# S5 matrices and rotation tables computed in the retention passes and reloaded per step

## The chip, the cores and the metric

The kernel runs on one core of a Trainium2 chip, as one launch. The metric is device time in microseconds (us); three runs of the kernel before gave 1194.45, 1194.66 and 1196.43, and 1194.66 is their median. Five engines work beside each other, each through its own instructions in order: TensorE (PE, with its weight loads as PEld), VectorE (DVE), ScalarE (ACT), GpSimd (POOL) and SyncE (SP), which here issues the DMAs.

## The reference

One block on x of 1024 x 1024 (sequence x model), float32, cut to what matters:

```python
h = rms_norm(x, norm1_g)
q, k, v, g_ret, u, g_s5 = split(h @ w_in)            # widths 512, 512, 4 x 1024
ret = retention(rotary(q), rotary(k), v, ret_gn_g) * silu(g_ret)   # 8 heads, chunks of 128
# S5 branch: 64 groups of 16 channels, 64 complex states each
dt = exp(log_dt);  abar = exp(a * dt)                # per group and state
bb = (abar - 1) / a * b
x_t = abar * x_(t-1) + bb @ u_t                      # associative scan over the sequence
y = gelu(Re(c @ x_t) + d * u)
y = y * sigmoid(y @ glu_w + glu_b)
x = x + concat(ret, y * silu(g_s5)) @ w_out
x = x + cross_attention(rms_norm(x), rms_norm(mem))  # 256 memory rows, 4 heads
out = rms_norm(x)
```

The recurrence of the S5 branch depends on the inputs only through u. Everything made from a, dt, b, c and d alone (the powers of abar, the input matrix, the output matrix, the local kernel) can be computed without u.

## The kernel before

The program runs through stages: loading and norm (to about 37 us), four retention passes i = 0 to 3 of two heads each, the S5 stretch, then the gate (`glups`), the second half of the output projection (`obps`), cross attention and its output (`wops`). A matrix product in full precision is three matmuls (`mm3`: high x high, high x low, low x high; L95 to L97), so a projection tile of 128 output columns over the whole sequence is 48 matmuls of 512 columns, into one of two large PSUM buffers (tag `big`); four small PSUM buffers (tag `sm`) serve everything else. Each weight block is loaded by SP, its high half `whi` made by ScalarE and its low half `wlo` by GpSimd for `w_u`, `w_gs` and `w_oa`, by VectorE otherwise; both have two buffers.

A retention pass projects k and q (`kps`, `qps`), v (`vps`) and the gate (`gps`), then runs `retention()`: scores and states (`st`, `R`), the outputs `ops`, the group norm (`ve`, three Newton steps `t_gn`, `nb`), the normalisation of `o` on ScalarE (L480), the product with the gate on VectorE (L481), the transposes `rtps` on TensorE and a store of `rt` to DRAM. The rope of q and k needs half rows swapped, which SP does by DMA (`sw_k`, `sw_q`).

The S5 stretch (about 370 to 720 us) projects u (`ups`, 8 tiles, each evacuated as `ut` and stored), the S5 gate (`gsps`, 8 tiles) and the first half of the output projection (`oaps`, 8 tiles, on `reth` and `retl`, the halves of the stored retention output). Beside these tiles stand the steps of the S5 branch, for b = 0 to 15 (four groups each): `s5_step()` emits `s5_out(b-2)`, `s5_state(b-1)` and `s5_prep(b)`.
- `s5_prep(b)` makes, on GpSimd, for every second b (each `ct`) the rotation tables `tab` by doubling; per b the small tiles B1, B2, C1 and `t1`; on VectorE the matrix W1 (L568, L570) and the output matrix VV (L577 to L579); on TensorE the transposes `mps` of W1 and the local kernel `kps` (L582); on ScalarE the copies Mi, `ktz` and the per-b copy CS of the tables (L597). Eight DMAs build Dm from `ktz`.
- `s5_state(b)` multiplies u by Mi (`Sps`), rotates (S, Sw) and scans (X); `s5_out(b)` rotates back (X2), multiplies by Dm and VV (`yps`), applies gelu and stores `yy`.

`s5_params()`, the powers of abar and the tables' start, is emitted in pass 1. A scheduler orders the instructions of every engine by a simulated timeline; each engine then runs its list in order and waits on semaphores, and a tile with one buffer makes its next writer wait for its last reader. SP's list is in order as well, so a store whose data is late holds the loads behind it.

Of the kernel before, what the change touches and what calls it, by code (L numbers as in the profile page):

```python
# [45 lines left out]
def block_kernel(ctx: ExitStack, tc: tile.TileContext, a: dict):  # L46
# [473 lines left out]
    NB = G // GB  # L520
    dms = []
    for z in range(2):
        dm = sb.tile([P, 2 * GB, P], F32, name=f"Dm{z}")
        g.memset(dm, 0.0)
        dms.append(dm)
    per_ct = {}

    def s5_prep(b):
        gs = slice(b * GB, b * GB + GB)
        ct, hb = b // 2, b % 2  # L530
        if hb == 0:
            raw = sb.tile([P, 2, 4, GB, 16], F32, tag="bcraw", name=f"bcraw{ct}", bufs=2)
            nc.sync.dma_start(out=raw, in_=a["s5_bc"][ct])
            tab = sb.tile([P, 2, GB, SC], F32, tag="tab", name=f"tab{ct}", bufs=2)
            g.tensor_copy(tab[:, 0, :, 0:16], rotC[:, ct])
            g.tensor_copy(tab[:, 1, :, 0:16], rotS[:, ct])
            scr = sb.tile([P, 256], F32, tag="tg", name=f"tg{ct}", bufs=1)
            rotate_double(tab[:, 0], tab[:, 1], 16, SC, scr, 4)
            ktz = sb.tile([16, 2 * GB, P], F32, tag="ktz", name=f"ktz_{ct}", bufs=1)
            per_ct[ct] = raw, tab, ktz  # L540
        raw, tab, ktz = per_ct[ct]
        raw = raw[:, hb]
        ks = slice(hb * GB, hb * GB + GB)
        B1 = sb.tile([P, GB, 16], F32, tag="B1", name=f"B1_{b}", bufs=2)
        B2 = sb.tile([P, GB, 16], F32, tag="B2", name=f"B2_{b}", bufs=1)
        C1 = sb.tile([P, GB, 16], F32, tag="C1", name=f"C1_{b}", bufs=1)
        tt = sb.tile([P, GB, 16], F32, tag="tt16", name=f"tt16_{b}", bufs=1)
        sh = [P, GB, 16]

        def fb(x):  # L550
            return bc(x[:, gs].unsqueeze(2), sh)
        g.tensor_tensor(B1, raw[:, 0], fb(FR), ALU.mult)
        g.tensor_tensor(tt, raw[:, 1], fb(FIs), ALU.mult)
        g.tensor_tensor(B1, B1, tt, ALU.add)
        g.tensor_tensor(B2, raw[:, 1], fb(FRs), ALU.mult)
        g.tensor_tensor(tt, raw[:, 0], fb(FI), ALU.mult)
        g.tensor_tensor(B2, B2, tt, ALU.subtract)
        g.tensor_scalar(C1, raw[:, 2], psgn, None, op0=ALU.mult)

        def pw(tab, n):  # L560
            return bc(tab[:, 0:n, gs].rearrange("p t g -> p g t").unsqueeze(3), [P, GB, n, 16])

        def ve(x, n):
            return bc(x.unsqueeze(2), [P, GB, n, 16])
        W1 = sb.tile([P, GB, 8, 16], F32, tag="W1", name=f"W1_{b}", bufs=1)
        t1 = sb.tile([P, GB, 9, 16], F32, tag="t1", name=f"t1_{b}", bufs=1)
        VV = sb.tile([P, GB, 9, 16], F32, tag="VV", name=f"VV_{b}", bufs=3)
        v.tensor_tensor(W1, pw(PR, 8), ve(B1, 8), ALU.mult)  # L568
        g.tensor_tensor(t1[:, :, 0:8], pw(PI, 8), ve(B2, 8), ALU.mult)
        v.tensor_tensor(W1, W1, t1[:, :, 0:8], ALU.add)  # L570
        mp = sm_ps([P, GB, P], "mps")
        for gi in range(GB):
            nc.tensor.transpose(mp[:, gi, :], W1[:, gi].rearrange("p t q -> p (t q)"), ident)
# [1 line left out]
        s.activation(Mi, mp, AF.Copy)
        t2 = sb.tile([P, GB, 9, 16], F32, tag="t1", name=f"t2_{b}", bufs=1)
        v.tensor_tensor(VV, pw(PR, 9), ve(C1, 9), ALU.mult)  # L577
        v.tensor_tensor(t2, pw(PI, 9), ve(raw[:, 3], 9), ALU.mult)
        v.tensor_tensor(VV, VV, t2, ALU.subtract)  # L579
        kp = sm_ps([P, P], "kps")  # L580
        for gi in range(GB):
            nc.tensor.matmul(kp[32 * gi:32 * gi + 16, :], B1[:, gi, :], VV[:, gi, 0:8, :].rearrange("p t q -> p (t q)"),  # L582
                             start=True, stop=True)
        for gi in range(GB):
            s.activation(ktz[:, hb * GB + gi, :], kp[32 * gi:32 * gi + 16, :], AF.Copy)
        dd = sb.tile([16, GB, 16], F32, tag="dd", name=f"dd_{b}", bufs=1)
        g.tensor_tensor(dd, bc(i16.unsqueeze(1), [16, GB, 16]), bc(d16[:, gs].unsqueeze(2), [16, GB, 16]), ALU.mult)
        g.tensor_tensor(ktz[:, ks, 0:16], ktz[:, ks, 0:16], dd, ALU.add)
        Dm = dms[ct % 2]
        if hb == 1:  # L590
            for j in range(8):
                r = 7 - j
                nc.sync.dma_start(out=Dm[16 * r:16 * r + 16, :, j * 16:P], in_=ktz[:, :, 0:P - j * 16])
        r0 = 64 * hb
        CS = sb.tile([P, 2, GB, SC], F32, tag="CS", name=f"CS_{b}", bufs=2)
# [495 lines left out]
```

## Time and profile before

| | |
|---|---|
| median of three runs | 1194.66 us |
| profiled execution | 1195.26 us, its span 1193.5 us |
| mean granted TensorE clock | 0.988 |
| busy: TensorE, VectorE, ScalarE, GpSimd | 1147.6, 677.6, 497.7, 297.9 us |
| chain that ended last | PE 73%, DVE 10%, POOL 5% |
| DMA | 137.67 MB, mean 115 GB/s |

The span is the time between the first and the last instruction; the device time has 1.8 us around it. The busy share is an average over stages with different limits, so the rows below are taken by stretch. Matmuls overlap in the records: one of 512 columns is noted with about 0.4 us, but the next starts 0.23 us later.

### The profile page before, as it was taken

The page shows a single profiled execution, that of the slowest core. Times are in us where ns is not written, and L with a number is a line of the kernel's source. Part 1 is how long each engine was busy: PE and PEld are TensorE (multiplying, and loading weights), DVE is VectorE, ACT ScalarE, POOL GpSimd, SP SyncE. Part 2 cuts the span into 40 slices and gives each one's busy share as a digit, 9 for nine tenths or more (in the row PEclk, how much of TensorE's full clock was granted, in tenths as well). Part 3 has the DMA queues.
Part 4 walks back from the last instruction along what each step waited for, and adds up shares of the span by engine and source line. Part 5 has one row for each costly group of instructions (what it writes and reads, how often), then busy time and mean ns, then how long its engine had stood idle before and what let it go on. Part 6 is the DMA issues. An engine that isn't in the chain of part 4 may idle for free.

```text
span 1193.5 us, 18220 instructions
## 1 busy us (share of the span) xinstructions
PE 1147.6 (96%) x7020; PEld 997.4 (84%) x7020; DVE 677.6 (57%) x1388; ACT 497.7 (42%) x983; POOL 297.9 (25%) x432
## 2 busy tenths in 40 slices
PE   9899999999999998899979999999999999999996
PEld 6898998998988877777757787888889988889996
DVE  8964414415114388999889746544545445554564
ACT  7322531522523135656655425223324444444452
POOL 1430000000112698889985200000330000000000
PEclk9899999999999998999989999999999999999999
DMA  6411311212211524343454459534444622222251
GB/s 218 114 37 54 89 54 37 98 62 55 88 54 54 176 72 127 122 125 110 149 160 160 125 187 284 173 124 135 134 150 164 206 76 72 71 71 71 90 194 71
DMA packets 74070, 137.67 MB, mean 115 GB/s; under 512 B 13952, under 2 KB 39808, under 8 KB 73984
## 3 DMA queue, kind: packets, MB, share of 16 engines
q1 hardware_dynamic: 73696, 136.38, 35.6%
q8 instruction: 55, 0.90, 0.3%
q14 instruction: 31, 0.25, 0.1%
q10 hardware_dynamic: 288, 0.14, 0.0%
HBM read 100.57 MB, written 29.36 MB: 109 GB/s over the span
## 4 chain that ended last, share of the span: by engine, by line
PE 73%; DVE 10%; POOL 5%; issue 4%; ACT 3%; DMA 3%; SPq 1%; DVEq 0%; ACTq 0%; POOLq 0%
PE vps L95 3%; PE vps L96 3%; PE vps L97 3%; PE gps L96 3%; PE wops L97 3%; PE wops L95 3%; PE wops L96 3%; PE gps L95 3%; PE gps L97 3%; PE glups L96 2%; PE qaps L97 2%; PE qaps L95 2%; PE qaps L96 2%; PE glups L97 2%; PE obps L96 2%
## 5 line engine op out<-in xcount | busy, mean ns | idle before, releaser
L75 POOL TENSOR_TENSOR wlo_w_u<-wraw_w_u,whi_w_u 128x512 fp32r<-128x512 f32 x16 | 20.7, 1325 | 286.2 <-ACT whi_w_u L74 286.2
L95 PE MATMUL wops<-whi_w_xo,o 128*128 128x256 f32 x256 | 74.1, 289 | 0.0
L95 PE MATMUL vps<-whi_w_v,hh 128*128 128x256 f32 x256 | 73.3, 286 | 0.6 <-ACT qs_k L288 0.6
L96 PE MATMUL vps<-wlo_w_v,hh 128*128 128x256 f32 x256 | 73.6, 287 | 0.0
L97 PE MATMUL vps<-whi_w_v,hl 128*128 128x256 f32 x256 | 73.4, 287 | 0.0
L97 PE MATMUL wops<-whi_w_xo,o 128*128 128x256 f32 x256 | 72.5, 283 | 0.0
L96 PE MATMUL wops<-wlo_w_xo,o 128*128 128x256 f32 x256 | 72.4, 283 | 0.0
L96 PE MATMUL gps<-wlo_w_g,hh 128*128 128x256 f32 x256 | 72.0, 281 | 0.0
L97 PE MATMUL gps<-whi_w_g,hl 128*128 128x256 f32 x256 | 72.0, 281 | 0.0
L95 PE MATMUL gps<-whi_w_g,hh 128*128 128x256 f32 x256 | 72.0, 281 | 0.0
L821 POOL TENSOR_TENSOR sq<-sq,sqx 128x1024 f32<-128x1024 f32 x7 | 19.1, 2723 | 190.2 <-ACT sqx L820 190.2
L95 PE MATMUL gsps<-hh,whi_w_gs 128*128 128x512 f32 x128 | 51.2, 400 | 7.3 <-DVE ut L678 7.3
L96 PE MATMUL oaps<-retl,whi_w_oa 128*128 128x512 f32 x128 | 51.9, 405 | 4.2 <-DVE retl L705 4.2
L95 PE MATMUL oaps<-reth,whi_w_oa 128*128 128x512 f32 x128 | 52.0, 408 | 0.0
L97 PE MATMUL oaps<-reth,wlo_w_oa 128*128 128x512 f32 x128 | 51.7, 404 | 0.0
L96 PE MATMUL gsps<-hl,whi_w_gs 128*128 128x512 f32 x128 | 51.3, 401 | 0.0
L96 PE MATMUL glups<-yl,whi_w_glu 128*128 128x512 f32 x128 | 50.7, 397 | 0.6 <-DVE yl L743 0.6
L97 PE MATMUL gsps<-hh,wlo_w_gs 128*128 128x512 f32 x128 | 51.1, 399 | 0.0
L96 PE MATMUL ups<-hl,whi_w_u 128*128 128x512 f32 x128 | 50.9, 398 | 0.0
L97 PE MATMUL ups<-hh,wlo_w_u 128*128 128x512 f32 x128 | 50.8, 397 | 0.0
L95 PE MATMUL ups<-hh,whi_w_u 128*128 128x512 f32 x128 | 50.8, 397 | 0.0
L95 PE MATMUL qaps<-h,whi_w_xq 128*128 128x512 f32 x128 | 50.7, 396 | 0.0
(395 smaller groups left out, 3627.2 us busy)
## 6 DMA issues: line engine op xcount, KB each, us to landing
yr<-y_d SPq DMA_DIRECT2D x16, 512.0 KB, 6.7
wraw_w_xq<-w_xq SPq DMA_DIRECT2D x16, 512.0 KB, 4.2
wraw_w_xo<-w_xo SPq DMA_DIRECT2D x16, 512.0 KB, 4.3
wraw_w_v<-w_v SPq DMA_DIRECT2D x8, 512.0 KB, 4.1
wraw_w_g<-w_g SPq DMA_DIRECT2D x8, 512.0 KB, 4.8
ret_d<-rt SPq DMA_DIRECT2D x16, 256.0 KB, 2.1
wraw_w_u<-w_u SPq DMA_DIRECT2D x8, 512.0 KB, 3.8
u_d<-ut SPq DMA_DIRECT2D x8, 512.0 KB, 3.5
```

The costliest lines, as they stand in the source:

```text
L75: lo_eng.tensor_tensor(lo[:, sl, :], raw[:, rs, :], hi[:, sl, :].bitcast(F32), ALU.subtract)
L95: nc.tensor.matmul(out, wh, xh, start=first, stop=False)
L96: nc.tensor.matmul(out, wh, xl, start=False, stop=False)
L97: nc.tensor.matmul(out, wl, xh, start=False, stop=last)
L821: g.tensor_tensor(sq2, sq2, sq, ALU.add)
```

## The change

`s5_params()` moves to the first pass, behind its last rope instruction. `s5_prep(b)` moves from the S5 steps to the ends of the passes (b = 0 to 3 behind the first, 4 to 8, 9 to 13 and 14, 15 behind the others) and stores Mi, VV, K (with d added in) and the tables to new DRAM arrays; its tiles lie in a pool `pr`, which is closed before the pools of the S5 stretch open. In its place `s5_load(b)` reloads them. The constant d is laid out so that one VectorE instruction adds it, K is copied by one ScalarE instruction instead of four, and `ut` is written by one instruction instead of eight. Some S5 tiles get a second buffer. SP's list has 129 more rows.

```diff
-        if i == 1:
-            s5_params()
+        if i == 0:
+            with tc.issue_after(last_rope[0].ins):
+                s5_params()
+        for b in range((0, 4, 9, 14)[i], (4, 9, 14, 16)[i]):
+            s5_prep(b)
     qctx.close()
+    prctx.close()
+    evctx = ExitStack()
+    ev = evctx.enter_context(tc.tile_pool(name="ev", bufs=2, reuse_waits="tile"))
...
+    def s5_tables(ct):
+        raw = pr.tile([P, 2, 4, GB, 16], F32, tag="bcraw", name=f"bcraw{ct}", bufs=2)
+        nc.sync.dma_start(out=raw, in_=a["s5_bc"][ct])
+        tab = pr.tile([P, 2, GB, SC], F32, tag="tab", name=f"tab{ct}")
...
+        rotate_double(tab[:, 0], tab[:, 1], 16, SC, scr, 4)
+        nc.sync.dma_start(out=a["tab_d"][ct], in_=tab)
+        zero = pr.tile([P, 2, 112], F32, tag="tg", name=f"z{ct}")
+        g.memset(zero, 0.0)
+        nc.sync.dma_start(out=a["k_d"][ct].rearrange("(h p) t -> p h t", h=2)[:, :, 0:112], in_=zero)
...
+        s.activation(Mi, mp, AF.Copy)
+        nc.sync.dma_start(out=a["mi_d"][b], in_=Mi)
...
+        nc.sync.dma_start(out=a["vv_d"][b], in_=VV.rearrange("p g t q -> p g (t q)"))
...
+        s.activation(K, kp, AF.Copy)
+        v.scalar_tensor_tensor(K[:, 0:16], i16, d4[:, b:b + 1], K[:, 0:16], op0=ALU.mult, op1=ALU.add)
+        nc.sync.dma_start(out=a["k_d"][ct][P * hb:P * hb + P, 112:112 + P], in_=K)
...
+    def s5_load(b):
         ct, hb = b // 2, b % 2
         if hb == 0:
+            us[ct] = sb.tile([P, 2 * GB, SC], F32, tag="U", name=f"U_{ct}", bufs=2)
+            nc.sync.dma_start(out=us[ct], in_=by_row("u_d", ct))
+            Dm = sb.tile([P, 2 * GB, P], F32, tag="Dm", name=f"Dm_{ct}", bufs=2)
+            kd = a["k_d"][ct].rearrange("(g c) t -> c g t", c=32)
+            for r in range(8):
+                nc.sync.dma_start(out=Dm[16 * r:16 * r + 16], in_=kd[0:16, :, 16 * r:16 * r + P])
+            per_ct[ct] = Dm
         Mi = sb.tile([P, GB, P], F32, tag="Mi", name=f"Mi_{b}", bufs=2)
+        nc.sync.dma_start(out=Mi, in_=a["mi_d"][b])
+        CS = sb.tile([P, 2, GB, SC], F32, tag="CS", name=f"CS_{b}", bufs=3)
         for z in range(2):
+            nc.sync.dma_start(out=CS[64 * z:64 * z + 64], in_=a["tab_d"][ct][64 * hb:64 * hb + 64])
+        VV = sb.tile([P, GB, 9 * 16], F32, tag="VV", name=f"VV_{b}", bufs=3)
+        nc.sync.dma_start(out=VV, in_=a["vv_d"][b])
...
-            for j in range(8):
-                v.tensor_tensor(ut[:, 7 - j], pv[:, :, j, :], rb[:, :, j, :], ALU.mult)
+            v.tensor_tensor(ut[:, ::-1], pv.rearrange("p n j c -> p j n c"), rb.rearrange("p n j c -> p j n c"), ALU.mult)
```

How the order moves is shown at three places. TensorE at the end of the fourth pass, before (`hh` and `hl` are the halves of the normed input, `ups` the u projection, `cp` the constants):

```order
L96 MATMUL ups<-hl_141,whi_w_u_12_3685 128x512
L97 MATMUL ups<-hh_140,wlo_w_u_12_3686 128x512
L485 MATMUL rtps<-cp,o_3493 128x128 x8
L95 MATMUL ups<-hh_140,whi_w_u_12_3685 128x512
L96 MATMUL ups<-hl_141,whi_w_u_12_3685 128x512
L97 MATMUL ups<-hh_140,wlo_w_u_12_3686 128x512
L95 MATMUL ups<-hh_151,whi_w_u_12_3685 128x512
L96 MATMUL ups<-hl_152,whi_w_u_12_3685 128x512
L97 MATMUL ups<-hh_151,wlo_w_u_12_3686 128x512
L95 MATMUL ups<-hh_151,whi_w_u_12_3685 128x512
L485 MATMUL rtps<-cp,o_3493 128x128 x8
L96 MATMUL ups<-hl_152,whi_w_u_12_3685 128x512
```

After, the same place (`W` is W1, `B` is B1; numbers 14 and 15 are b):

```order
L97 MATMUL ups<-hh_196,wlo_w_u_11_4000 128x512
L95 MATMUL ups<-hh_196,whi_w_u_11_3999 128x512
L96 MATMUL ups<-hl_197,whi_w_u_11_3999 128x512
L97 MATMUL ups<-hh_196,wlo_w_u_11_4000 128x512
L559 MATMUL rtps<-cp,o_4253 128x128 x16
L460 MATMUL mps<-cp,W_14_4477 128x128 x4
L470 MATMUL kps<-VV_4479,B_14_4465 32x128 x4
L460 MATMUL mps<-cp,W_15_4517 128x128 x4
L470 MATMUL kps<-VV_4519,B_15_4505 32x128 x4
L95 MATMUL ups<-hh_133,whi_w_u_12_4553 128x512
L96 MATMUL ups<-hl_134,whi_w_u_12_4553 128x512
L97 MATMUL ups<-hh_133,wlo_w_u_12_4554 128x512
```

Before, matmuls of the third `ups` tile stand around the two groups of eight `rtps`, and no prep; now the 16 `rtps` and the `mps` and `kps` of b = 14 and 15 stand in one piece, and the third `ups` tile begins behind them.

VectorE at the same place, before (`L678` is the evacuation of an `ups` tile):

```order
L118 TENSOR_TENSOR t_gn_3614<-rs_3610 128x16
L119 SCALAR_TENSOR_TENSOR t_gn_3614<-t_gn_3614,ve_3609 128x16
L120 SCALAR_TENSOR_TENSOR rs_3610<-t_gn_3614,rs_3610 128x16
L476 SCALAR_TENSOR_TENSOR nb_3611<-mv_3494,rs_3610 128x16
L481 TENSOR_TENSOR o_3493<-o_3493,silu_3014 128x1024 x2
L678 TENSOR_TENSOR ut_3880<-ups,rstd_b 128x128 x8
L678 TENSOR_TENSOR ut_4007<-ups,rstd_b 128x128 x8
L577 TENSOR_TENSOR VV_3928<-PR,C_0_3917 128x576
L568 TENSOR_TENSOR W_0_3926<-PR,B_0_3915 128x512
```

After:

```order
L118 TENSOR_TENSOR t_gn_4374<-rs_4370 128x16
L119 SCALAR_TENSOR_TENSOR t_gn_4374<-t_gn_4374,ve_4369 128x16
L120 SCALAR_TENSOR_TENSOR rs_4370<-t_gn_4374,rs_4370 128x16
L550 SCALAR_TENSOR_TENSOR nb_4371<-mv_4254,rs_4370 128x16
L555 TENSOR_TENSOR o_4253<-o_4253,silu_3774 128x1024 x2
L455 TENSOR_TENSOR W_15_4517<-PR,B_15_4505 128x512
L457 TENSOR_TENSOR W_15_4517<-W_15_4517,t_15_4518 128x512
L474 SCALAR_TENSOR_TENSOR K_4501<-cp,K_4501 128x16
L474 SCALAR_TENSOR_TENSOR K_4541<-cp,K_4541 128x16
L692 TENSOR_TENSOR ut_4616<-ups,rstd_b 128x8x128
L692 TENSOR_TENSOR ut_4668<-ups,rstd_b 128x8x128
L692 TENSOR_TENSOR ut_4734<-ups,rstd_b 128x8x128
```

The evacuations `ut` that stood before and inside the norm's end now stand behind it, behind W1 of b = 15 and the K tiles of both.

SP between the first and the second pass, before (`wraw` are the weights' loads, the digit behind a name counts the passes from 0):

```order
L70 DMA wraw_w_g1_40_1241<-w_g 128x1024
L70 DMA wraw_w_g1_41_1247<-w_g 128x1024
L292 DMA sw_k1_1168<-qs_k1_1166 32x1024 x4
L70 DMA wraw_w_kq2_50_1465<-w_kq 128x1024
L292 DMA sw_q1_1228<-qs_q1_1226 32x1024 x4
L70 DMA wraw_w_kq2_51_1471<-w_kq 128x1024
```

After, the same place (`tab_d` and `k_d` are the new arrays, `z` is a tile of zeros):

```order
L70 DMA wraw_w_g1_40_1641<-w_g 128x1024
L70 DMA wraw_w_g1_41_1647<-w_g 128x1024
L417 DMA tab_d_65<-tab0_1289 128x1024
L420 DMA k_d_66<-z0_1312 128x2x112
L294 DMA sw_k1_1568<-qs_k1_1566 32x1024 x4
L417 DMA tab_d_65<-tab1_1397 128x1024
L420 DMA k_d_66<-z1_1420 128x2x112
L417 DMA tab_d_65<-tab2_2303 128x1024
L420 DMA k_d_66<-z2_2326 128x2x112
L70 DMA wraw_w_kq2_50_1865<-w_kq 128x1024
L294 DMA sw_q1_1628<-qs_q1_1626 32x1024 x4
L70 DMA wraw_w_kq2_51_1871<-w_kq 128x1024
```

The rope swaps `sw_k1` and `sw_q1` of the second pass's k and q, which had only weight loads ahead of them, now stand behind the store of the first table and behind those of the first three.

## Rows read from the trace of the kernel before

**Rows 1.** Busy time by stretch: us, PE, PEld, DVE, ACT, POOL, PEclk, DMA share, GB/s
```profile
235.00:318.00 83.00, 83.00 (x627) 76.27 (x627) 27.48 (x75) 28.95 (x67) 0.00 (x0) 1.00 0.21 64
420.00:720.00 300.00, 270.08 (x1438) 218.80 (x1437) 246.46 (x324) 155.47 (x267) 206.72 (x327) 0.97 0.44 136
452.60:458.50 5.90, 5.90 (x27) 5.71 (x28) 2.69 (x10) 2.36 (x5) 5.62 (x6) 0.52 0.60 156
603.30:608.80 5.50, 5.50 (x14) 4.32 (x15) 5.50 (x11) 3.88 (x9) 1.33 (x6) 0.53 0.80 270
51.30:54.20 2.90, 0.06 (x2) 0.08 (x1) 2.90 (x27) 0.00 (x0) 0.00 (x0) 1.00 0.00 0
54.20:58.50 4.30, 4.30 (x26) 4.30 (x27) 3.96 (x26) 3.14 (x10) 0.00 (x0) 0.65 0.01 2
```

**Rows 2.** TensorE's waits, 369 to 720 us: total, times, longest us
```profile
PE gsps L95 <- DVE ut L678: 7.3, 1, 7.3
PE yps L646 <- DVE X L642: 5.4, 5, 1.4
PE oaps L96 <- DVE retl L705: 4.2, 1, 4.2
```

**Rows 3.** VectorE's instruction groups, 420 to 720 us: busy us, mean ns | idle before
```profile
L568 DVE TENSOR_TENSOR W<-PR,B 128x512 f32<-128x512 f32 x14 | 12.6, 901 | 0.6 <-POOL B L554 0.4 <-PE mps L573 0.2
L570 DVE TENSOR_TENSOR W<-W,t 128x512 f32<-128x512 f32 x14 | 11.3, 810 | 5.6 <-POOL t L569 5.6
L577 DVE TENSOR_TENSOR VV<-PR,C 128x576 f32<-128x576 f32 x13 | 14.2, 1094 | 11.4 <-PE yps L646 11.4
L578 DVE TENSOR_TENSOR t<-PI,bcraw 128x576 f32<-128x576 f32 x15 | 18.6, 1238 | 0.1
L579 DVE TENSOR_TENSOR VV<-VV,t 128x576 f32<-128x576 f32 x15 | 21.3, 1417 | 0.1
L716 DVE TENSOR_TENSOR xo<-oaps,xo 128x1024 f32<-128x1024 f32 x7 | 8.5, 1213 | 6.5 <-PE oaps L97 6.5
L678 DVE TENSOR_TENSOR ut<-ups,rstd_b 128x128 f32<-128x128 f32 x24 | 5.0, 275 | 0.0
```

**Rows 4.** Timeline at the end of the fourth pass: start us, us, engine
```profile
369.15 0.49 PE L460 MATMUL ops<-R,rot_q 64*128 64x128 f32 x4
369.91 0.40 PE L97 MATMUL ups<-hh,wlo_w_u 128*128 128x512 f32 x1
370.14 0.40 PE L95 MATMUL ups<-hh,whi_w_u 128*128 128x512 f32 x1
374.35 5.11 POOL L75 TENSOR_TENSOR wlo_w_u<-wraw_w_u,whi_w_u 128x512 fp32r<-128x512 f32 x4 [28.86 <-ACT whi_w_u L74]
380.16 0.18 DVE L476 SCALAR_TENSOR_TENSOR nb<-mv,rs 128x16 f32<-128x16 f32 x1
380.43 6.28 ACT L480 ACTIVATE o<-o,nb,rs 128x128 f32<-128x128 f32 x16 [4.59 <-DVE nb L476]
386.74 1.23 DVE L481 TENSOR_TENSOR o<-o,silu 128x1024 f32<-128x1024 f32 x1 [1.86 <-ACT o L480]
```

**Rows 5.** Timeline at 432 us, and line L626: ns min/median/max
```profile
432.91 7.43 DVE L626 TENSOR_TENSOR Sw<-Sw,CS 128x512 f32<-128x512 f32 x1
432.44 2.54 POOL L75 TENSOR_TENSOR wlo_w_gs<-wraw_w_gs,whi_w_gs 128x512 fp32r<-128x512 f32 x2
...
L626 DVE TENSOR_TENSOR Sw<-Sw,CS x14: 673/680/7428, 432.9 to 662.6; 128x512 f32<-128x512 f32 x14
```

**Rows 6.** Timeline at the end of the first pass
```profile
134.56 1.23 DVE L295 TENSOR_TENSOR sw_q<-sw_q,sinT 128x1024 f32<-128x1024 f32 x1 [3.25 <-DMA sw_q<-qs_q]
136.96 2.35 DVE L481 TENSOR_TENSOR o<-o,silu 128x1024 f32<-128x1024 f32 x2
139.52 1.03 PE L485 MATMUL rtps<-cp,o 128*128 128x128 f32 x8
```

**Rows 7.** DMA issues of the page: count, KB each, median us to landing
```profile
ret_d<-rt SPq DMA_DIRECT2D x16, 256.0 KB, 2.1
```

More of the change, by code (lines that the diff above doesn't have):

```diff
@@ L314, in s5_params @@
     def s5_params():
-        scratch = [ev.tile([P, 16, G], F32, tag="ut", name=f"s5scr{z}") for z in range(2)]
+        scratch = pr.tile([P, 16, G], F32, tag="tab", name="s5scr")
         taken = [0]
         def tmp(name):
-            z = taken[0]
             taken[0] += 1
-            return scratch[z // 16][:, z % 16, :]
+            return scratch[:, taken[0] - 1, :]
         ar, ai, dt, k, k1, r, p, mg, th = (tmp(f"s5{z}") for z in
@@ new lines, in s5_prep, with fb, pw, ve @@
+    def s5_prep(b):
+        gs = slice(b * GB, b * GB + GB)
+        ct, hb = b // 2, b % 2
+        if hb == 0:
+            s5_tables(ct)
+        raw = per_ct[ct][:, hb]
+        B1 = pr.tile([P, GB + 1, 16], F32, tag="B1", name=f"B1_{b}", bufs=2)
+        B2 = pr.tile([P, GB, 16], F32, tag="B2", name=f"B2_{b}")
+        C1 = pr.tile([P, GB, 16], F32, tag="C1", name=f"C1_{b}")
+        tt = pr.tile([P, GB, 16], F32, tag="tt16", name=f"tt16_{b}")
+        sh = [P, GB, 16]
+        def fb(x):
+            return bc(x[:, gs].unsqueeze(2), sh)
+        g.memset(B1[:, GB, :], 0.0)
+        g.tensor_tensor(B1[:, 0:GB], raw[:, 0], fb(FR), ALU.mult)
+        g.tensor_tensor(tt, raw[:, 1], fb(FIs), ALU.mult)
+        g.tensor_tensor(B1[:, 0:GB], B1[:, 0:GB], tt, ALU.add)
+        g.tensor_tensor(B2, raw[:, 1], fb(FRs), ALU.mult)
+        g.tensor_tensor(tt, raw[:, 0], fb(FI), ALU.mult)
+        g.tensor_tensor(B2, B2, tt, ALU.subtract)
+        g.tensor_scalar(C1, raw[:, 2], psgn, None, op0=ALU.mult)
+        def pw(tab, n):
+            return bc(tab[:, 0:n, gs].rearrange("p t g -> p g t").unsqueeze(3), [P, GB, n, 16])
+        def ve(x, n):
+            return bc(x.unsqueeze(2), [P, GB, n, 16])
+        W1 = pr.tile([P, GB, 8, 16], F32, tag="W1", name=f"W1_{b}")
+        t1 = pr.tile([P, GB, 8, 16], F32, tag="t1", name=f"t1_{b}")
+        VV = pr.tile([P, GB, 9, 16], F32, tag="VV", name=f"VV_{b}", bufs=2)
+        t2 = pr.tile([P, GB, 9, 16], F32, tag="t2", name=f"t2_{b}")
+        v.tensor_tensor(W1, pw(PR, 8), ve(B1[:, 0:GB], 8), ALU.mult)
+        g.tensor_tensor(t1, pw(PI, 8), ve(B2, 8), ALU.mult)
+        v.tensor_tensor(W1, W1, t1, ALU.add)
+        mp = sm_ps([P, GB, P], "mps")
+        for gi in range(GB):
+            nc.tensor.transpose(mp[:, gi, :], W1[:, gi].rearrange("p t q -> p (t q)"), ident)
+        Mi = pr.tile([P, GB, P], F32, tag="Mi", name=f"Mi_{b}", bufs=2)
+        s.activation(Mi, mp, AF.Copy)
+        nc.sync.dma_start(out=a["mi_d"][b], in_=Mi)
+        v.tensor_tensor(VV, pw(PR, 9), ve(C1, 9), ALU.mult)
+        v.tensor_tensor(t2, pw(PI, 9), ve(raw[:, 3], 9), ALU.mult)
+        v.tensor_tensor(VV, VV, t2, ALU.subtract)
+        nc.sync.dma_start(out=a["vv_d"][b], in_=VV.rearrange("p g t q -> p g (t q)"))
+        kp = sm_ps([P, P], "kps")
+        for gi in range(GB):
+            nc.tensor.matmul(kp[32 * gi:32 * gi + 32, :], B1[:, gi:gi + 2, :].rearrange("p g q -> p (g q)"),
+                             VV[:, gi, 0:8, :].rearrange("p t q -> p (t q)"), start=True, stop=True)
+        K = pr.tile([P, P], F32, tag="K", name=f"K_{b}", bufs=2)
+        s.activation(K, kp, AF.Copy)
+        v.scalar_tensor_tensor(K[:, 0:16], i16, d4[:, b:b + 1], K[:, 0:16], op0=ALU.mult, op1=ALU.add)
+        nc.sync.dma_start(out=a["k_d"][ct][P * hb:P * hb + P, 112:112 + P], in_=K)
@@ L520, in block_kernel @@
[L520 to L529, printed above, removed]
+    def s5_load(b):
         ct, hb = b // 2, b % 2
         if hb == 0:
[L532 to L573, printed above, removed]
-        Mi = sb.tile([P, GB, P], F32, tag="Mi", name=f"Mi_{b}", bufs=2)
[L575 to L590, printed above, removed]
-            for j in range(8):
[L592 to L595, printed above, removed]
@@ L665, in s5_step @@
         if b < NB:
-            preps[b] = s5_prep(b)
+            preps[b] = s5_load(b)
     for gi in range(4):
@@ L1055, in host_arrays @@
     out["ident"] = np.eye(P, dtype=f32)
-    out["i16"] = np.eye(16, dtype=f32)
+    out["i16"] = c(np.tile(np.eye(32, 16, dtype=f32), (4, 1)))
     out["cmask"] = (lt[:, None] <= lt[None, :]).astype(f32)
```

45 lines of the change are left out of this document (25 added, 20 removed).

## The prediction

> **What bounds the kernel now.** I first read the busy time, the clock and the other engines' load by stretch [rows 1], then TensorE's waits in the stretch from 369 us on [rows 2], then what one S5 preparation costs VectorE there [rows 3], and last the single places whose order the change moves [rows 4 to 6] and what a transfer takes [rows 7].
>
> TensorE runs in order and sets the end. In a retention pass (235 to 318 us) it is busy 83.00 of 83.00 us, VectorE 27.48, GpSimd not at all. From 420 to 720 us it is busy 270.08 of 300.00, so it waits 29.9 us; VectorE is busy 246.46 and GpSimd 206.72 [rows 1]. It waits mostly for VectorE: 7.3 us for a ut tile (the longest), 5.4 for X2 (five times), 4.2 for retl [rows 2]. Two of these waits also cost clock. [...] What the S5 stretch loses is therefore 29.9 + 5.4 = 35.3 us.
>
> **What leaves the stretch.** Per b, W1 costs VectorE 12.6/14 + 11.3/14 us, VV 14.2/13 + 18.6/15 + 21.3/15: 0.90 + 0.81 + 1.09 + 1.24 + 1.42 = 5.5 us [rows 3], 16 of them. Of VectorE's 246 us in 300 some 80 go. GpSimd loses the tables, the B and C tiles, t1 and the K/D adds, and keeps the wlo halves; ScalarE loses the CS copies and the four K copies per b. What VectorE keeps per step (ut or gg, the S and X group, gelu) fits in the 14 us that TensorE needs for a tile of 48 matmuls at 0.23 us [rows 4] and a step's Sps and yps (some 24 instructions of 128 columns, eight in 1.03 us [rows 6]). ut in one instruction reads 1024 PSUM elements per partition as L716 does, 1.2 us [rows 3], against eight pieces of 0.28; the pieces give the upper bound, 2.2, and a 512-wide instruction the lower, 0.7 [rows 5]; I take 1.2. I take the 35.3 us as gone, and then add what is late next.
>
> **What comes back inside the stretch.** (a) The wait for retl at 599 us has another cause: retl, made of two SBUF tiles, stands beside GpSimd's run of four wlo_w_oa. That stays: +4.2 us [rows 2], without its half clock (bounds 0 and 4.2 + 2.6). (b) Short waits for X2 where four wlo fall into a step's S-to-X2 chain: eight weight blocks, 0 to 1.4 us each (the longest wait for X2 in [rows 2]); I take +3, bounds 0 and 11.
>
> How long wlo holds VectorE: Sw at 432.91 us took 7.43 us, where the median of its line is 0.68, and the two wlo that were running when it started ended at 434.98 [rows 5]. It waited through the run of GpSimd instructions behind them too. [...]
>
> **The end of the fourth pass.** This is the term against the change. In the order of after, only 17 ups matmuls stand between the last ops and the 16 rtps, then mps/kps of b = 14 and 15, then the third ups tile. Both large PSUM buffers are full by then, and VectorE frees the first with ut0 only behind nb3, both o products, W1_15, K_14 and K_15. In before, ut tiles stand between these and TensorE never waits there. Worked out from the last ops (369.6 us in before, my zero) by [rows 4]:
> - 17 matmuls at 0.23: TensorE is done at 3.9.
> - nb ends at 380.34 in before, 10.7. Of this 0.8 was a ut evacuation that now comes later; 9.9. The four wlo_w_u that hold it back (374.35, 5.11 us) stay, since whi and wlo of that block wait for the end of the first 96 matmuls in both.
> - ScalarE's 16 o normalisations take 6.28: halves at 13.0 and 16.2. VectorE's products 1.23 each: 14.3 and 17.4. Each eight rtps take 1.03 [rows 6]: done at 18.5.
> - mps and kps of 14, four 128-column instructions each, 1.0: 19.5. W1 has one buffer, so W1_15 starts behind mps_14: 19.0 + 0.90 + 0.81 = 20.7. mps_15, kps_15: 21.7. K_15 through ScalarE and VectorE 0.8, ut0 1.2: 23.7.
> TensorE works 2.1 + 2.0 of the 19.8 us between: it waits 15.7 us. What comes after runs on half clock as in [rows 1]: 2.8 us after the restart, and 1.5 on the rtps, mps and kps in between. Sum +20.0. Bounds: 11, if the wlo come after nb (4.5 less) and no clock is lost before the restart; 27, if ut0 also waits for a run of wlo and rtps for GpSimd's o operands.
>
> **The passes.** TensorE's work there grows by what leaves the stretch: nothing. VectorE has 55 us free in 83 [rows 1]. Fourteen preps stand in the passes behind the rtps of the pass before, most 39 rows of the order apart (39 x 83.0/627 = 5.2 us, [rows 1]), the next W1 behind the last mps. At the 5.5 us of [rows 3] plus 0.2 for K a prep is 0.5 us longer than that; with all five at the median of a 512-wide instruction [rows 5] it is 3.6: between 0 and 14 x 0.5 = 7, I take +1.5, since GpSimd has no wlo in passes two and three.
> The first pass has less room at its end: sw_q lands at 134.56 and VectorE waits for it 3.25 us, then come rot_q and the two o products, 136.96 to 139.31, and rtps starts at 139.52 with no wait [rows 6]: the slack is 0.2 to 1.4 us. In after GpSimd runs the tables there, and on SP's queue sw_k1 stands behind the store of tab0, and sw_q1 behind those of tab1 and tab2 and a weight load. I put tab2's end by GpSimd's contended durations at about 125 us, 0 to 5 us on either side, near enough to be late: four products of 1.23 that each wait a GpSimd instruction, or sw_q1 late by that. +3, bounds 0 and 8. SP issues 129 more DMAs in all (64 stores, the reloads), spread over 600 us; where they stand behind data that is not there, they hold the next weight load, which has a whole projection of slack.
>
> **The start.** s5_params goes behind the last rope instruction; before, its first 20 us stood between the xr sums. TensorE waited 2.9 us from 51.3 for the r1 chain and then had a clock of 0.65 for 4.3 us, 1.5 us lost [rows 1]. Params still alternate with the chain, which starts sooner: -3, bounds -4.4 and +2 (the chain later by the rope).
>
> **Sum.** Profiled execution 1195.3 (span 1193.5): 1195.3 - 35.3 + 4.2 + 3 + 20.0 + 1.5 + 3 - 3 = 1188.7. The median is 0.6 below the profiled run: **1188 us**. The terms' bounds together hardly meet; half of each way gives 1181 to 1196.
>
> **Rivals.**
> 1. *The tail is short.* wlo of the third block comes after nb, VectorE then is never blocked there, and the retl wait shrinks as GpSimd has no preps ahead of wlo_w_oa. For it: GpSimd is nearly idle then. Against it: whi waits for the same matmuls as before. 1188 - 9 (tail at 11) - 4.2 - 4.5 (passes without loss) = **1170**.
> 2. *The passes become bound by VectorE and GpSimd: slower.* Preps take VectorE 5.7 us as in [rows 3], and the pass's other work (27.5 us in 83) comes between at half its mean density, 0.8: 6.5 against 5.2, 14 x 1.3 = 18, where 1.5 is counted; and the chain at the first pass's end is late by 5 more. 1188 + 16.5 + 5 = **1209**; half of it gives 1199. It decides once a prep needs more than 5.2 us. For it: slack of 0.2 us at rtps, stores ahead of the rope swaps. Against it: GpSimd idle in passes, VectorE at a third.
> 3. *Reloads are late.* CS, Mi, VV and Dm stand on SP's one queue behind yy stores, whose data comes at a step's end. A 256 KB transfer lands 2.1 us after its issue [rows 7], and is issued a step ahead. If SP is held up to the step's start, Sps waits about 0.5 us in 16 steps, **1196**; if all of 2.1, 1222. Against it: 13.9 us of lead. That the work would not leave the stretch is excluded: the order of after has it in the passes.
>
> **Chances.** Forecast 0.48, rival 1 0.21, rival 2 0.20, rival 3 0.11. About 0.2%, 2.4 us, is what a measurement of this kernel can tell from no change. The forecast's own range is 1181 to 1196: 0.38 faster, 0.08 within, 0.02 slower. Rival 1 is faster, rival 2 slower, rival 3 half within and half slower. Faster 0.59, same 0.14, slower 0.27. The range takes in rival 1 and most of rival 2: 1168 to 1205.
>
> **What the profile after would show.** Right: TensorE over 97% busy in the gsps and oaps tiles, VectorE at two thirds there; one stretch of some 20 us at the end of the fourth pass in which TensorE has only rtps, mps and kps, ended by ut0, with half clock behind it; passes still 83 us. Wrong: TensorE waiting for W1, VV or K in the passes, or for o at the first rtps (rival 2); waits of Sps for CS or Mi (rival 3); the third ups tile starting less than 15 us after the last ops (rival 1). A pass longer than 84 us would undo the sum first.

## The result, and the profile after

| | before, same chip | after |
|---|---|---|
| median | 1195.36 us | 1185.4 us (1184.52 to 1186.16, four runs) |
| profiled execution, span | 1195.26, 1193.5 us | 1184.93, 1183.1 us |
| mean granted TensorE clock | 0.988 | 0.980 |

The ratio is 0.9916, 95% interval 0.9899 to 0.9933: faster by 0.8%, against a forecast of 1188 us. The number fits; the runs below show that the terms behind it do not all fit, and that what the edit was read for is not what made the kernel faster.

First the stretches that answer to [rows 1], in the kernel after: us, then PE, PEld, DVE, ACT, POOL busy (with counts), PEclk, DMA share, GB/s.

```profile
49.41:53.83 4.42, 0.01 (x2) 0.04 (x1) 4.42 (x33) 0.00 (x0) 0.00 (x0) 1.00 0.01 3
...
139.16:149.84 10.68, 0.00 (x1) 0.01 (x1) 4.71 (x4) 3.03 (x11) 9.35 (x18) 0.67 0.54 140
149.84:160.00 10.16, 10.16 (x79) 9.83 (x80) 4.43 (x7) 3.43 (x6) 7.41 (x19) 0.84 0.49 182
440.00:700.00 260.00, 259.60 (x1329) 220.07 (x1328) 143.31 (x231) 96.86 (x160) 48.41 (x50) 1.00 0.78 230
403.20:424.00 20.80, 6.14 (x42) 4.79 (x41) 10.73 (x16) 12.41 (x28) 5.08 (x6) 0.64 0.35 130
424.00:430.00 6.00, 6.00 (x15) 4.73 (x16) 1.03 (x1) 0.00 (x0) 0.00 (x0) 0.53 0.72 188
```

From 440 to 700 us TensorE is busy 259.60 of 260.00 us at a full granted clock, VectorE 55% of the time (two thirds were forecast), and the DMA share has gone up from 0.44 to 0.78. The second and third rows are the end of the first pass, the last two the end of the fourth, where TensorE waited for nothing of the kind before. TensorE's waits, answering to [rows 2] (total, times, longest us), say the same:

```profile
PE rtps L559 <- DVE o L555: 22.1, 3, 10.7
PE mps L460 <- DVE W L457: 4.7, 3, 3.3
PE bcps L128 <- issue: 4.4, 1, 4.4
PE ups L95 <- DVE ut L692: 1.9, 1, 1.9
...
PE mps L460 <- DVE K L474: 1.4, 1, 1.4
...
PE oaps L96 <- DVE retl L719: 0.4, 1, 0.4
```

The waits for ut in the stretch and for X2 are gone, retl's shrank from 4.2 to 0.4 us; new are the two of some 10 us for `o`. One stretch is also worth a look, since nothing in it was edited: from the first `glups` to the end the work is the same 2745 matmuls. The stretch before, and after:

```profile
718.12:1184.33 466.21, 465.56 (x2745) 411.01 (x2743) 241.75 (x490) 191.83 (x388) 23.49 (x10) 1.00 0.39 129
```
```profile
712.40:1173.97 461.57, 460.65 (x2745) 408.22 (x2743) 235.59 (x484) 186.48 (x382) 23.42 (x10) 1.00 0.38 124
```

After takes 4.6 us less for it, and not by waits: the matmuls themselves follow each other faster. The same is seen in the passes; `gps` before and after, duration in ns as minimum, median and maximum:

```profile
L97 PE MATMUL gps<-whi_w_g,hl x256: 279/281/285, 66.9 to 338.0; 128*128 128x256 f32 x128
```
```profile
L97 PE MATMUL gps<-whi_w_g,hl x256: 276/276/582, 66.8 to 367.7; 128*128 128x256 f32 x128
```

From the start of one to the start of the next, 256 columns take 115 to 122 ns before and mostly 113 or 114 after, in this stage. I summed, over all matmuls of 256 and 512 columns, what the start-to-start time is above 113.33 ns per 256 columns, about the shortest that is frequent (only distances less than 16 ns above it, so that waits stay out; some 5470 of the 7020 matmuls count). This sum, called the excess from here on, is 28.6 us before and 13.9 after. These 14.7 us are more than the 10.4 us by which the span shrank.

### The profile page after: what moved, and what is told of

Read it like the earlier page. It is cut to its first block, busy times and chain, and to the rows that moved or that the text cites. A ratio compares the mean times of both kernels' runs of the same rounds, so it can differ in the third digit from the quotient of the medians.

```text
span 1183.1 us, 18360 instructions
## 1 busy us (share of the span) xinstructions
PE 1133.3 (96%) x7020; PEld 992.1 (84%) x7020; DVE 639.1 (54%) x1348; ACT 451.6 (38%) x903; POOL 284.1 (24%) x422
## 4 chain that ended last, share of the span: by engine, by line
PE 58%; DMA 3%; DVE 2%; ACT 1%; issue 0%; POOL 0%; DVEq 0%; ACTq 0%; POOLq 0%
PE wops L96 3%; PE wops L97 3%; PE wops L95 3%; PE qaps L96 3%; PE qaps L97 2%; PE glups L95 2%; PE qaps L95 2%; PE glups L97 2%; PE obps L96 2%; PE obps L95 2%; PE obps L97 2%; PE glups L96 2%; PE gsps L97 2%; PE gsps L96 2%; PE gsps L95 2%; PE oaps L97 2%
## 5 line engine op out<-in xcount | busy, mean ns | idle before, releaser
L97 PE MATMUL qaps<-h,wlo_w_xq 128*128 128x512 f32 x128 | 50.6, 395 | 0.0
L95 PE MATMUL qaps<-h,whi_w_xq 128*128 128x512 f32 x128 | 50.5, 394 | 0.0
L96 PE MATMUL qaps<-h,whi_w_xq 128*128 128x512 f32 x128 | 50.4, 394 | 0.0
L95 PE MATMUL glups<-yh,whi_w_glu 128*128 128x512 f32 x128 | 50.3, 394 | 0.0
```

The costliest lines, as they stand in the source:

```text
L95: nc.tensor.matmul(out, wh, xh, start=first, stop=False)
L96: nc.tensor.matmul(out, wh, xl, start=False, stop=False)
L97: nc.tensor.matmul(out, wl, xh, start=False, stop=last)
```

## The experiments: is it the edit or the placement?

As the two programs are built, the weights' tiles begin 96 bytes past a multiple of 256 in SBUF, the memory that holds the tiles, before, and 160 after; `hh` begins at the same address in both. The change made the constants' tile 192 bytes smaller and the DMA reserve (`dynamic_dma_scratch_size`) 15360 bytes smaller, and everything behind moved. The first two runs shrink the reserve in before, the second with a filler of the same size in its place.

```diff
-    nc = bacc.Bacc("TRN2", target_bir_lowering=False, num_devices=1)
+    nc = bacc.Bacc("TRN2", target_bir_lowering=False, num_devices=1, dynamic_dma_scratch_size=1024)
```
and, in the second,
```diff
+    fill = ctx.enter_context(tc.tile_pool(name="fill", bufs=1, reuse_waits="tile"))
+    nc.gpsimd.memset(fill.tile([P, 3840], F32, name="filler")[0:1, 0:1], 0.0)
```

> The kernel before with one edit: the DMA reserve at the bottom of SBUF is 1024 bytes instead of the default 16384, so the weight tiles lie 15360 bytes lower and the activations stay where they were. In the trace of after, a matmul follows the last one 113 to 118 ns (256 columns) or 227 to 229 ns (512 columns) later, in before 118 to 119 and 232 almost everywhere; summed over the matmuls of the projections that is 14.7 us. Theory A (placement): the pitch falls with the addresses alone. Then this kernel takes 1195 - 13 = about 1182 us, with the waits of before unchanged (29.9 us from 420 to 720 us). Theory B (the order and the lighter load of VectorE and GpSimd make the pitch): 1195 us, pitch 118.5 and 232 as in before.

> As the run before, and a filler tile of 15360 bytes below the constants, so that every other tile is back at its old address (weights at 22368) while the reserve stays small. Theory A (placement): about 1195 us, pitch 118.5 and 232 ns. If the reserve's size itself does it, whatever the addresses: about 1182 us, pitch as with the small reserve. Theory B: 1195 us in both runs.

Measured: 1195.75 us, ratio 1.0000 (0.9991 to 1.0008), excess 28.9; with the filler 1196.03, 1.0002 (0.9991 to 1.0012), excess 28.7. Neither moves anything, so the reserve and the filler as such cost nothing. But 15360 is 60 x 256: the weights stayed at 96 past a multiple of 256. What had not been tried is the 192 bytes. So the next runs put a filler of 64 or 128 bytes ahead of the constants in before, and of 64, 128 or 192 bytes in after (the same two lines with another size). The filler adds one memset to GpSimd's list; otherwise every engine has the same instructions in the same order as without it.

> The kernel before with a filler of 64 bytes per partition ahead of the constants: weights at 160, activations at 224 within 256 bytes, as in after. Theory A2: excess 14 us instead of 28.6, time 1195.4 - 14.5 = about 1181 us, with all waits of before. Theory B: 1195 us.

> The kernel before with a filler of 128 bytes per partition: weights and activations both at 224 within 256 bytes. The tiles of the second half of the output projection lie like the weights in before as in after (difference 0), and there the excess is 0.1 us in both. Theory A2: excess under 6 us, time about 1195.4 - 24 = 1171 us. Theory B: 1195 us.

> After with a filler of 64 bytes per partition: weights and activations both at 224 within 256 bytes. Theory A2: excess under 5 us instead of 13.9, time 1185.4 - 10 = about 1175 us. Theory B: 1185 us.

> After with a filler of 128 bytes per partition: weights at 32, activations at 224 within 256 bytes, the fourth of the four places in steps of 64. Measured so far, as excess in ns per matmul of 512 and of 256 columns: weights at 96 5.5 and 5.3, at 160 2.4 and 0 or 4.4 in turns, at 224 under 1 and 6.5. If the excess depends on the distance alone, 32 is as 160 (64 bytes apart in the other direction): summed 14 us, about 1185 us. If it depends on the direction too: anything else between 5 and 30 us of excess, 1176 to 1201 us.

> After with a filler tile of 192 bytes per partition ahead of the constants, nothing else. The two runs that moved the weights by 15360 bytes, a multiple of 256, left the matmul pitch as it was; the whole change moves them by 15552, because the constant tile is 192 bytes narrower as well. Theory A2 (the pitch depends on where weights and activations lie against each other within 256 bytes): before has weights at 96 and activations at 224, after 160 and 224. This filler puts after back to 96 and 224: pitch 118.5 and 232 ns, summed excess 28 us instead of 13.9, time 1185.4 + 14.5 = about 1200 us, slower than before. Theory B (order and load): 1185 us, excess 14.

Each ratio is to runs of before on the same chip.

| weights past 256 | kernel | median, us | ratio to before | excess, us |
|---|---|---|---|---|
| 96 | before | 1195.36 | 1 | 28.6 |
| 96 | after + 192 bytes | 1197.22 | 1.0017 (1.0005 to 1.0028) | 29.1 |
| 160 | before + 64 bytes | 1185.66 | 0.9917 (0.9896 to 0.9938) | 14.2 |
| 160 | after | 1185.40 | 0.9916 (0.9899 to 0.9933) | 13.9 |
| 224 | before + 128 bytes | 1192.09 | 0.9970 (0.9961 to 0.9979) | 20.6 |
| 224 | after + 64 bytes | 1185.42 | 0.9926 (0.9899 to 0.9953) | 19.3 |
| 32 | after + 128 bytes | 1196.22 | 1.0002 (0.9990 to 1.0014) | 26.9 |

The first four rows decide. A filler of 64 bytes, with no other edit, takes as much off before as the whole change does; and the change with the weights where they were in before is slower by 0.17%. The rows of the unchanged stages confirm it, before + 64 and after + 192:

```profile
711.12:1172.85 461.73, 460.56 (x2745) 407.16 (x2743) 241.49 (x490) 191.88 (x388) 23.48 (x10) 1.00 0.40 130
```
```profile
722.15:1186.92 464.77, 464.77 (x2745) 411.32 (x2743) 235.41 (x484) 186.12 (x382) 23.44 (x10) 1.00 0.38 123
```

Over all the runs of this document this stretch takes 460.3 to 463.1 us with 160 (six kernels) and 464.8 to 466.5 with 96 (five), whatever the edit; with 224 it takes 462.1 and with 32 465.1. With 224 the 256-column distances are mostly 119 to 121 ns and the 512-column ones 226 to 228; with 32 they are mostly 117 or 118 and 231 to 236.

For 224, where weights and activations begin at the same place, the expectation failed: the 512-column matmuls became short, the 256-column ones did not, so the excess was 20.6 and 19.3 us and not under 6. For 32 it was 26.9 and not 14, so the distance between weights and activations alone, whatever its sign, does not set it. One stage tells what counts for 512 columns. In `obps` the activations (`ssmhi`, `ssmlo`) begin at the same place as the weights in all seven kernels of the table, and its excess is 0.1 us in each of them. In `glups`, with the same shapes and activations at 224, it is 2.2 us with the weights at 96, 0.9 with 160, 0.1 or less with 224 and 2.6 with 32. There the place of the weights against that of the activations counts, and not the weights' alone. After + 64 has 5.4 us more excess than after and the same time; its waits at the start and at the first transposes were 2.6 and 8.9 us where after has 4.4 and 10.7, which is 3.6 of them. Before + 128 has 8.0 us less excess than before and a span only 5.3 us shorter; TensorE is idle for 2.5 us more (48.4 against 45.9). Why a matmul's distance changed with where its operands begin was not settled.

## The experiments: what the edit itself does

The `ut` instruction alone, in before:

```diff
-            for j in range(8):
-                v.tensor_tensor(ut[:, 7 - j], pv[:, :, j, :], rb[:, :, j, :], ALU.mult)
+            v.tensor_tensor(ut[:, ::-1], pv.rearrange("p n j c -> p j n c"), rb.rearrange("p n j c -> p j n c"), ALU.mult)
```

> The kernel before with only the evacuation of ut in one instruction; all tiles keep their addresses. If the instruction itself matters where TensorE waits 7.3 us for ut, behind VectorE instructions held up by GpSimd: at most 1 us per tile on eight tiles, the wait for ut and its half clock partly gone, 1189 to 1193 us. If that wait is the blocked VectorE queue ahead of ut (as I read the trace of before), 1194 to 1196 us, no change.

Measured: 1188.94 us, 0.9937 (0.9923 to 0.9952), with an excess of 28.7, so this is not placement. TensorE's idle time from the last `ops` to the first `glups` falls from 29.3 to 22.5 us; before, and this run:

```profile
369.37:718.12 348.75, 319.41 (x1670) 258.94 (x1668) 270.55 (x395) 170.00 (x299) 237.05 (x378) 0.98 0.44 136
```
```profile
367.92:710.91 342.99, 320.50 (x1669) 260.76 (x1668) 267.61 (x346) 170.80 (x300) 240.63 (x378) 0.98 0.46 139
```

The 7.3 us wait for ut is not among TensorE's waits any more. The scheduler put the instructions of all five engines in a somewhat different order for this edit, and what the instruction itself is worth was not told apart from that. On top of it the rest of the change, with the weights at the same place, costs 8 to 10 us (1197.22 against 1188.94, or 0.8% by the ratios).

Next, the waits in the passes. In e3 the preparations stand behind the rope of the following pass, with the tables' stores kept behind the swaps on SP; the two at the fourth pass's end stay.

```diff
         qT = rope(proj_t(w, 1, hT, name="qps"), f"q{i}")
+        for b in range((0, 0, 4, 9)[i], (0, 4, 9, 14)[i]):
+            s5_prep(b)
...
-        nc.sync.dma_start(out=a["tab_d"][ct], in_=tab)
+        with tc.issue_after(last_swap[0].ins):
+            nc.sync.dma_start(out=a["tab_d"][ct], in_=tab)
...
-        for b in range((0, 4, 9, 14)[i], (4, 9, 14, 16)[i]):
-            s5_prep(b)
+    for b in range(14, 16):
+        s5_prep(b)
```

> After with one edit: the preparations are emitted behind the next pass's rope and each table's store is pinned behind that pass's swap DMAs on SP; the groups per pass and the tail stay. Theory C (SP's queue): the 10.7 us wait at the first rtps came from sw_q1 standing behind the store of the third table (issued at 137.2 us instead of 128.1). Then the wait is under 1.5 us, the half clock behind it goes too, and the time is 1185.4 - 11 = about 1174 us. Rival (GpSimd's tables slow VectorE's norm chain): the wait stays at 8 us or more and the time is 1183 to 1186.

Measured: 1189.28 us, 0.9944 (0.9928 to 0.9959), so 4 us slower than after and not 11 faster. The wait at the first `rtps` is gone, as theory C had it, but the waits at the `mps`, 4.7 us in after, have grown by nearly as much:

```profile
PE mps L462 <- DVE W L459: 14.5, 6, 4.3
PE rtps L561 <- DVE o L557: 11.3, 2, 10.2
```

The remaining wait of 10.2 us at `rtps` is the tail. e5 has e3's order with groups of 5, 5 and 6 and none behind the fourth pass; e4 has after's order with such groups and nothing else:

```diff
-        for b in range((0, 4, 9, 14)[i], (4, 9, 14, 16)[i]):
+        for b in range((0, 5, 10, 16)[i], (5, 10, 16, 16)[i]):
```

> The edit of the run before, and the groups are b = 0 to 4, 5 to 9 and 10 to 15 in the second, third and fourth pass, none behind the fourth, so that the pool of the ut tiles finds its memory free early and ut stands ahead of the norm's end again. Theory D (the tail is bound by the order that puts ut0 behind preparations 14 and 15): its waits of 14.7 us and some 4 us of half clock go: 1174 - 18 = about 1156 us. Rival (the wait only moves, to W1 or ut in the denser fourth pass): 5 to 12 us of it come back, 1161 to 1168.

> After with one edit: the groups of preparations behind the passes are b = 0 to 4, 5 to 9, 10 to 15 and none behind the fourth; tables and stores stay as in after. Theory D (the tail is the order that puts ut0 behind preparations 14 and 15): its 14.7 us of waits and some 4 us of half clock go, the 10.7 us at the first rtps stays: 1185.4 - 18 = about 1167 us. Rival (denser passes give it back at mps): 5 to 12 us come back, 1172 to 1179.

Measured: e5 1176.37 us, 0.9823 (0.9804 to 0.9843), slower than both its theories; e4 1170.76, 0.9782 (0.9758 to 0.9807), between them. The two preparations at the end of the fourth pass thus cost 14.6 us of after, against the 20 forecast for that place; a part goes back to the passes, where two more preparations stand (`mps` waits 8.0 us instead of 4.7; in e5, 19.9). The longest waits of e4:

```profile
PE rtps L559 <- DVE o L555: 10.7, 1, 10.7
PE mps L460 <- DVE W L457: 8.0, 4, 3.1
```

The last run lets GpSimd issue the 16 stores that it is the source of, in e4:

```diff
-        nc.sync.dma_start(out=a["tab_d"][ct], in_=tab)
+        nc.gpsimd.dma_start(out=a["tab_d"][ct], in_=tab)
...
-        nc.sync.dma_start(out=a["k_d"][ct].rearrange("(h p) t -> p h t", h=2)[:, :, 0:112], in_=zero)
+        nc.gpsimd.dma_start(out=a["k_d"][ct].rearrange("(h p) t -> p h t", h=2)[:, :, 0:112], in_=zero)
```

> Like the version without preparations behind the fourth pass (e4: 1170.8), but the 16 stores that have a rotation table or the tile of zeros as their source are issued by GpSimd, which made them, and not by SP. Theory: the 10.7 us that TensorE waits at the first transposes is SP standing at the store of the third table (issued 135.6 in e4) with the swap of q behind it; then the swap is issued near 128, as in before, the sine product of q near 135, the first rtps near 138.8, and the time is 1170.8 - 10 to 11.5, about 1160. Rival 1: the wait is given back at the mps as in e3, because the preparations' VectorE instructions are then what ends late: rtps early, mps waits of the first pass from 5 to 8 or 12 us, about 1168. Rival 2: it is GpSimd's and VectorE's contention at the pass's end that makes o late, not the queue: swap early, o products still behind 145, about 1171. [...]

Measured: 1168.73 us, 0.9780 (0.9761 to 0.9799), the fastest median here, though not told apart from e4. Its timeline at that place (start us, us, engine):

```profile
126.88 2.59 SPq L294 DMA_DIRECT2D sw_q<-qs_q  x4
...
132.95 1.46 DVE L297 TENSOR_TENSOR sw_q<-sw_q,sinT 128x1024 f32<-128x1024 f32 x1 [1.27 <-DMA sw_q<-qs_q]
...
152.04 0.73 POOL L313 TENSOR_TENSOR tab<-tab,tg 128x256 f32<-128x256 f32 x1
...
155.21 0.31 POOL L438 TENSOR_TENSOR B<-bcraw,FR 128x64 f32<-128x64 f32 x1
...
161.77 1.09 PE L460 MATMUL mps<-cp,W 128*128 128x128 f32 x4 [8.97 <-DVE W L457]
```

The theory was right on the queue: the swap is issued at 126.88 us instead of 137.37 in e4, and the first transposes no longer wait 10.7 us. Rival 1 was right on the time: B of the next preparation stands behind a table on GpSimd (the fourth, which ends at 152.77 us), W1 behind B, and TensorE now waits 9.0 us at an `mps`. SP was the last to be late, GpSimd the next.

## Why the prediction came out right in its number

**What left the stretch (-35.3, then +7.2 back).** Right, and more than forecast. Of the 35.3 us, 5.4 are an estimate, 0.48 x 5.90 + 0.47 x 5.50, from the clocks of 0.52 and 0.53 in [rows 1]. Waits and half clock are gone (259.60 of 260.00 us busy from 440 us on, at 1.00), and of the 4.2 us for retl and 3 for X2 that were to come back only 0.4 did, for retl (its longest instruction takes 1.23 us, before 6.14 with a median of 1.31). But 6.8 us of the waits go in e6 as well, where the preparations stay in the stretch; for that part the move was not needed. The blocked rotation of [rows 5], up to 7.43 us long before, is now at most 1.77:

```profile
L641 DVE TENSOR_TENSOR Sw<-Sw,CS x16: 674/696/1770, 452.7 to 647.2; 128x512 f32<-128x512 f32 x16
```

The reloads that the third rival feared have no wait in the list: the transfers land 4.5 us after their issue, twice the 2.1 us of [rows 7], and are early enough. SP issues 518 DMAs in after and 390 in before, 128 more and not 129.

```profile
CS<-tab_d SPq DMA_DIRECT2D x32, 256.0 KB, 4.5
...
VV<-vv_d SPq DMA_DIRECT2D x16, 288.0 KB, 4.5
```

**The end of the fourth pass (+20.0).** Right step by step. After's timeline there, answering to [rows 4]:

```profile
398.61 0.49 PE L534 MATMUL ops<-R,rot_q 64*128 64x128 f32 x4
...
403.76 4.93 POOL L75 TENSOR_TENSOR wlo_w_u<-wraw_w_u,whi_w_u 128x512 fp32r<-128x512 f32 x4 [28.55 <-ACT whi_w_u L74]
...
403.89 1.17 DVE L118 TENSOR_TENSOR t_gn<-rs 128x16 f32<-128x16 f32 x1
...
407.54 1.19 DVE L550 SCALAR_TENSOR_TENSOR nb<-mv,rs 128x16 f32<-128x16 f32 x1
...
412.06 1.23 DVE L555 TENSOR_TENSOR o<-o,silu 128x1024 f32<-128x1024 f32 x1 [3.33 <-ACT o L554]
...
413.43 1.94 PE L559 MATMUL rtps<-cp,o 128*128 128x128 f32 x8 [10.23 <-DVE o L555]
...
421.07 0.63 PE L460 MATMUL mps<-cp,W 128*128 128x128 f32 x4 [1.37 <-DVE K L474]
...
423.96 0.80 PE L95 MATMUL ups<-hh,whi_w_u 128*128 128x512 f32 x1 [1.91 <-DVE ut L692]
```

From the end of the last `ops` (399.10) nb ends after 9.6 us (9.9 forecast), the first product of `o` after 14.2 (14.3), and the third ups tile starts after 24.9 (23.7). The waits are 10.23 + 1.16 + 1.37 + 1.91 = 14.7 us (15.7), and the lower clock takes 0.47 x 6.00 behind and 0.36 x 6.14 in between, 5.0 us (4.3): 19.7. Here each VectorE instruction from 403.89 to nb took about one GpSimd instruction's time (1.17 to 1.19 us instead of the 0.17 or 0.18 of the Newton step before, beside four wlo in 4.93 us, 1.23 each). In [rows 5] it was not one instruction's time: Sw took 7.43 us, to 440.34, beside a run of GpSimd instructions without a gap from 432.44 to 440.65. Why the two places differ was not shown.

**The end of the first pass (+3, bounds 0 and 8).** This is the step that failed. The wait and the lower clock behind it are 10.7 + 0.16 x 10.16 = 12.3 us. Answering to [rows 6]:

```profile
123.49 0.24 POOL L413 COPY tab<-rotC 128x64 f32<-128x64 f32 x1 [2.47 <-DMA tab_d<-tab]
...
135.26 0.32 SPq L417 DMA_DIRECT2D tab_d<-tab  x1
135.30 0.29 POOL L419 MEMSET z<- 128x224 f32 x1
...
137.20 2.73 SPq L294 DMA_DIRECT2D sw_q<-qs_q  x4
...
145.10 1.46 DVE L297 TENSOR_TENSOR sw_q<-sw_q,sinT 128x1024 f32<-128x1024 f32 x1 [11.36 <-DMA sw_q<-qs_q]
148.04 2.88 DVE L555 TENSOR_TENSOR o<-o,silu 128x1024 f32<-128x1024 f32 x2
```

The mechanism was named in the prediction: the swap stands on SP behind the third table's store. Its size was not: I put the table's end at 125 us, 0 to 5 to either side, and it came at 135.2. With one buffer for the table, GpSimd also waits for the store to land before it starts the next table (2.47 us for the second, in the first line; 14.8 us in six such waits over all eight tables). The product of q that the late swap holds up stands ahead of both products of `o` on VectorE.

**The passes (+1.5, bounds 0 and 7).** The remaining waits at mps are 1.2 and 3.3 us (173.8 and 351.7 us), and the clock is 0.55 for 7 us behind the second: 7.6, just outside the bounds as well.

```profile
355.04:362.00 6.96, 6.96 (x39) 6.25 (x40) 3.92 (x5) 0.84 (x2) 6.41 (x12) 0.55 0.24 92
```

That a preparation needs more of VectorE than its 5.2 us is not why. VectorE's groups in the passes, answering to [rows 3]:

```profile
L455 DVE TENSOR_TENSOR W<-PR,B 128x512 f32<-128x512 f32 x14 | 12.7, 907 | 23.6 <-PE mps L460 21.9 <-POOL B L440 1.7
L464 DVE TENSOR_TENSOR VV<-PR,C 128x576 f32<-128x576 f32 x14 | 12.6, 902 | 3.7 <-POOL C L444 3.7
...
L466 DVE TENSOR_TENSOR VV<-VV,t 128x576 f32<-128x576 f32 x14 | 11.7, 834 | 0.0
L457 DVE TENSOR_TENSOR W<-W,t 128x512 f32<-128x512 f32 x14 | 10.9, 780 | 7.9 <-POOL t L456 7.9
...
L465 DVE TENSOR_TENSOR t<-PI,bcraw 128x576 f32<-128x576 f32 x13 | 10.0, 766 | 0.4
```

The five means sum to 4.2 us, not 5.5. Where VectorE waits inside a preparation it is for GpSimd (7.9 us for t1, 3.7 for C1, 1.7 for B1), which the prediction counted as free in the second and third pass. The 21.9 us for `mps` are W1's one buffer, as forecast. So the second rival had the places, and both of its signs came (TensorE waiting for W1 in the passes and for `o` at the first rtps), but its price, VectorE's time, was not the cause.

One sign of being right, passes of 83 us, was wrong by the prediction's own working, which moves the mps and kps into the passes. From the first matmul of k's projection to the next pass's, the second and third pass took 100.4 and 86.2 us, and the fourth 92.8 to the first `ups` (82.9 each before). This did not undo the sum: some 13 us of it are the mps and kps of fourteen preparations at about 0.9 us each, which the stretch no longer has, and 20 are the waits and the lower clock of this term and the one before, less what the placement takes off.

**The start (-3).** Wrong in sign by the wait (4.4 us instead of 2.9), but nothing was lost: `bcps` starts at 53.83 (54.15 before) and the first `gps` at 66.6 (66.7). TensorE came to it earlier and waited longer. The term is 0.

**The sum.** -35.3 + 0.4 + 19.7 + 12.3 + 7.6 + 0 = +4.7, where the prediction had -6.6. The run that has the weights at the old place gives +2.6 by its span (1196.1 to 1193.5), 2 us less; by the matmuls' start times, `yps` and `Sps` of the stretch take some 41 us instead of 45.8 beside the idle time counted here, which no term has. Then the placement, in no term and in no rival, took off the 11.8 us between after + 192 and after. So the forecast of 1188 was met by an error of 9 to 11 us in the terms and one of about 12 that was not in them, of opposite sign. That is luck: with the weights at their old place the change took 1197.22 us, 9 more than forecast, and was no faster than before. The tail (rival 1 at 1170) was not short. e4, which takes it away, comes to that time, but its weights begin at 160 as in after, so what the placement gives is in it; e4 with the weights at 96 was not run.

## What to carry to other kernels

Compare two versions of a tuned kernel at the same placement of its large tiles, or with a few bytes of filler in both, before a per cent is put down to an edit; the sign to look for is a stage that was not edited and got faster (here 466.21 to 461.57 us for the same 2745 matmuls). Work that is moved into slack has to be followed through every engine and queue that it passes, to the end of the run of instructions ahead of it: here a store on SP waited for GpSimd until 135.26 us, and the swap behind it went out at 137.20. Where several things are late by about as much, as SP and then GpSimd at the first pass's end, removing one shows the next and not the gain: in e7 the 10.7 us at `rtps` became 9.0 at an `mps`.
